# A 31-tap depthwise convolution in three blocks of a fused model: two of six channel chunks move to ScalarE and GpSimd

## The chip, the cores and the metric

The kernel runs on one core of one Trainium2 chip. The metric is the device time of one execution in microseconds. Before the change, three runs took 1864.44, 1865.39 and 1867.44 us, so the median is 1865.39 us. One further execution was taken with the hardware profiler; all rows below come from it.

## The reference, cut to what matters

The model is a chain of three blocks over a sequence of 256 tokens with 1024 channels, in float32. The change lies in the first half of the third block ("3a"), in its convolution mixer:

```
proj = h @ w_in
a    = proj[..., :768] + b_glu[:768]
gate = proj[..., 768:1536] + b_glu[768:]
q_mem = proj[..., 1536:]
u = a * sigmoid(gate)
c = depthwise_conv(pad_left(u, 30), dw_w) + dw_b     # 31 taps per channel, 768 channels
c = silu(layer_norm(c, ln_g, ln_b))
m = memory_attention(q_mem, memq_g, mem_k, mem_v)    # 4 heads of 64
x = x + concat(c, m) @ w_out
```

Each output channel of the convolution is the sum of 31 products, each of one channel of `u`, shifted by one to 31 tokens, with one weight of that channel. After it come a SwiGLU, then block 3b (sliding-window attention and a mixture of eight experts).

## The kernel before, in words

Activations lie with channels on the 128 partitions and tokens on the free axis; a tile is 128 x 2 x 256, two chunks of 128 channels. Weights stream from HBM into a ring of 1 MB buffers (`raw`, issued on SyncE's queue). For precise float32 products ScalarE (ACT) rounds a weight piece into `whi` (L305) and VectorE (DVE) subtracts it into `wlo` (L306); `mm3` (L325) makes three products of each pair. A piece has 1024 columns, and each of the two tags has four buffers.

The convolution's 768 channels are six chunks, (p, c) with p from 0 to 2 and c 0 or 1. `block3a` (L1122) runs over p: two linear layers make `a` and `gate` of the pair (L1153, L1155), ACT takes the sigmoid (L1163), DVE multiplies into `u` (tile `cu`, 32 columns of zeros ahead of 256). The 31 taps of a chunk are split:

- Taps 0 to 17 run on DVE in `taps` (L1140): the first is a `tensor_scalar` with the bias (L1148), each further one a `scalar_tensor_tensor` that reads the shifted `u` and the running sum `conv`, and writes the sum back (L1150). These are 18 dependent instructions per chunk, 108 in all.
- Taps 18 to 30 (`PE_TAPS = 13`) run on TensorE (PE): ACT scales the identity by the weight column into a 128 x 128 diagonal `dg` (L1181, six buffers, no dependence on the data), and PE multiplies `u` by it into the PSUM tile `cv` (L1182). These are 78 diagonals and 78 float32 products (two records each in the trace).
- DVE adds `cv` to `conv`, once for each p (L1186).

After that come the memory attention (L1187 and L1188), which needs nothing of the convolution, the mean over channels (`mu`, L1191), the subtraction (L1196), the variance, `rs` (L1203), the normalisation (L1208), SiLU (L1210), and the output projection (L1213), which begins with the memory attention's chunks.

The order of the instructions on each engine isn't written out. A list scheduler orders them at compile time: of the instructions that it holds to be ready, an engine takes the one that was written first in the program, by the scheduler's own estimate of durations. On the chip every engine then runs its list in that order, and an instruction that waits holds up all that are behind it. The tiles of `bpool_tile` (L591) come from a pool of four buffers, 128 x 2 x 288.

GpSimd (POOL) has 30 instructions in the whole kernel: fills of constants and zeros, and a few DMA issues.

Of the kernel before, what the change touches and what calls it, by code (L numbers as in the profile page):

```python
# [15 lines left out]
AF = mybir.ActivationFunctionType  # L16
OP = mybir.AluOpType
# [10 lines left out]
GROUPS = ((0,), (1,), (2, 3), (4, 5), (6, 7))  # L28
TAGS = ("u", "u", "x2", "u", "x2")
HEAD = 2  # L30
PE_TAPS = 13
EARLY = 7
PRE = 2
KEEP = (0, 72, 81)
# [174 lines left out]
class Build:  # L209
# [912 lines left out]
    def block3a(self):  # L1122
        nc, a = self.nc, self.a
        gg = self.small("gg", 8)
        nc.vector.tensor_tensor(gg, self.col("fin_g", 0, 8), self.col("cv_g", 0, 8), op=OP.mult)
        h = self.gained(self.x, lambda c: gg[:, c:c + 1])
        rs1 = self.rms_row(self.sum_sq(self.x), "rs1")
        acc = self.sum_sq(self.x, lambda c: self.col("fin_g", c))
        for i in range(2):
            nc.vector.tensor_tensor(acc, acc, rs1, op=OP.mult)  # L1130
        rs = self.rms_row(acc)
        for j in range(4):
            for c in range(2):
                nc.vector.scalar_tensor_tensor(self.x[j][:, c, :], self.x[j][:, c, :], self.col("fin_g", 2 * j + c),
                                               rs1, op0=OP.mult, op1=OP.mult)
        nc.vector.tensor_tensor(rs, rs, rs1, op=OP.mult)
        w = a["cv_w_in"]
        us, cs, todo = [], [], []

        def taps(n):  # L1140

            for _ in range(min(n, len(todo))):
                p, c, j = todo.pop(0)
                cc = 2 * p + c
                src, o = us[p][:, c, j + 2:j + 258], cs[p][:, c, :]
                wc = self.col("dw_w", cc * 31 + j)
                if j == 0:
                    nc.vector.tensor_scalar(o, src, wc, self.col("dw_b", cc), op0=OP.mult, op1=OP.add)  # L1148
                else:
                    nc.vector.scalar_tensor_tensor(o, src, wc, o, op0=OP.mult, op1=OP.add)  # L1150

        for p in range(3):
            pa_ = self.linear(w, 2 * p, h)  # L1153
            taps(EARLY)
            pg = self.linear(w, 2 * p + 1, h)  # L1155
            u = self.bpool_tile("cu")
            nc.gpsimd.memset(u[:, :, 0:32], 0.0)
            sg = self.stile("sg").rearrange("p (a b) -> p a b", a=2)
            self.scaled(sg, pg, rs)
            self.scaled(u[:, :, 32:288], pa_, rs)  # L1160
            for c in range(2):
                cc = 2 * p + c
                self.gate_act(sg[:, c, :], sg[:, c, :], AF.Sigmoid, bias=self.col("glu_b", 6 + cc))  # L1163
                nc.vector.scalar_tensor_tensor(u[:, c, 32:288], u[:, c, 32:288], self.col("glu_b", cc), sg[:, c, :],
                                               op0=OP.add, op1=OP.mult)
            us.append(u)
            cs.append(self.unit("conv"))
            todo += [(p, c, j) for c in range(2) for j in range(31 - PE_TAPS)]
            taps(EARLY)
        pq = self.linear(w, 6, h)  # L1170
        q = self.unit("mq")
        self.scaled(q, pq, rs)
        self.exp_set()
        for p in range(3):
            t = cs[p]
            pc = self.pb("cv")
            for c in range(2):
                cc = 2 * p + c
                for i, j in enumerate(range(31 - PE_TAPS, 31)):
                    dg = self.medium("dg")  # L1180
                    nc.scalar.activation(dg, self.con("ident"), AF.Copy, scale=self.col("dw_w", cc * 31 + j))  # L1181
                    nc.tensor.matmul(pc[:, c * 256:(c + 1) * 256], dg, us[p][:, c, j + 2:j + 258], start=i == 0,  # L1182
                                     stop=i == PE_TAPS - 1, skip_group_check=True)
                while todo and todo[0][:2] <= (p, c):
                    taps(1)
            nc.vector.tensor_tensor(t, t, pc.rearrange("p (a b) -> p a b", a=2), op=OP.add)  # L1186
        self.head_rms(q.rearrange("p a b -> p (a b)"), q, self.g8[:, 0:1])  # L1187
        om = self.mem_attention(q)  # L1188
        pm = self.pa("mu")
        for cc in range(6):  # L1190
            self.stats_mm(pm, cs[cc // 2][:, cc % 2, :], cc == 0, cc == 5)  # L1191
        mu = self.stile("mu", 256)
        nc.scalar.activation(mu, pm[:, :256], AF.Copy, scale=1.0 / 768)
        pv = self.pa("var")
        for p in range(3):
            nc.vector.tensor_tensor(cs[p], cs[p], mu.rearrange("p (a b) -> p a b", a=1).to_broadcast([128, 2, 256]),  # L1196
                                    op=OP.subtract)
            sq = self.stile("sq")
            nc.scalar.activation(sq, cs[p].rearrange("p a b -> p (a b)"), AF.Square)
            for c in range(2):  # L1200
                self.stats_mm(pv, sq[:, c * 256:(c + 1) * 256], p == 0 and c == 0, p == 2 and c == 1)
        rs = self.stile("rs", 256)
        self.rsqrt(rs, pv[:, :256], 1.0 / 768, "e5")  # L1203
        act = []
        for p in range(3):
            for c in range(2):
                cc = 2 * p + c
                nc.vector.scalar_tensor_tensor(cs[p][:, c, :], cs[p][:, c, :], self.col("ln_g", cc), rs,  # L1208
                                               op0=OP.mult, op1=OP.mult)
                self.gate_act(cs[p][:, c, :], cs[p][:, c, :], AF.Silu, bias=self.col("ln_b", cc))  # L1210
            act.append(self.split(cs[p], "cn"))
        self.exp_set()
        self.out_proj(a["cv_w_out"], self.chunks([om]), self.chunks(act), self.add_x)  # L1213
        self.dump("x2b", self.x)
        h = self.gained(self.x, lambda c: self.col("cvf_g", c))
        rs = self.rms_row(self.sum_sq(self.x))
        f = []
        for j in range(11):
            pg = self.linear(a["cv_w_gate"], j, h)
            pu = self.linear(a["cv_w_up"], j, h)  # L1220
            t, v = (self.stile(n).rearrange("p (a b) -> p a b", a=2) for n in ("sg", "su"))
            self.scaled(t, pg, rs)
            self.gate_act(t, t, AF.Silu)
            self.scaled(v, pu, rs)
            nc.vector.tensor_tensor(t, t, v, op=OP.mult)
            f.append(self.split(t, "f", "u2" if j < 4 else "u"))
        self.exp_set()
        for j in range(4):
            self.add_x(j, self.linear(a["cv_w_down"], j, self.chunks(f)))
# [466 lines left out]
```

## Time and profile before

| What | Value |
|---|---|
| median of three runs | 1865.39 us |
| profiled execution, own time | 1858.88 us |
| its span | 1857.0 us |
| busy: PE, DVE, ACT, POOL | 1817.5, 1207.7, 960.9, 10.8 us |
| granted clock of TensorE over the span | 0.995 |
| convolution stretch, first tap on DVE to the last sum | 605.1 to 663.9 us |

The span is the time from the first to the last instruction in the profile; the execution's own time is 1.9 us longer. Busy shares are means over stages of different character: from 1060 us on, among the experts, the DMA engines are busy for 0.99 of the time, and in the convolution for 0.37 and 0.11.

### The profile page before, as it was taken

To read this page: it belongs to the slowest core of one execution; us is meant where nothing else is said; L and a number is where in the kernel's file an instruction comes from. 1 tells how busy PE (TensorE), PEld (TensorE's weight loads), DVE (VectorE), ACT (ScalarE), POOL (GpSimd) and SP (SyncE) were. 2 spreads that over 40 slices of the span, in tenths; PEclk is the share of its full clock that TensorE was granted. 3 is DMA by queue.
4 is the path that set the end of the run, shared out by engine and by line. 5 is a ranking of instruction groups with operands and counts; after the bars stand their busy time and mean duration, and the time that the engine had idled before them with its cause. 6 is when DMAs were issued, how large, how long until landed. Compare 5 with 4: busy or idle time off the path is not lost. (4 is left out here: it accounts for less than half of the span.)

```text
span 1857.0 us, 30774 instructions
## 1 busy us (share of the span) xinstructions
PE 1817.5 (98%) x12304; PEld 1505.6 (81%) x12304; DVE 1207.7 (65%) x1814; ACT 960.9 (52%) x1429; POOL 10.8 (1%) x30
## 2 busy tenths in 40 slices
PE   7999999999999999999998999999999999999997
PEld 7989998989999979999877766766676666676674
DVE  7689787666467977665577654656555655565563
ACT  5545555555455675454565644545454444444451
POOL 0000000000000000000000000000000000000000
PEclk9999999999999999999999999999999999999999
DMA  9766467345554215555524899999999999999995
GB/s 307 256 251 227 183 227 286 129 144 204 182 182 169 108 56 194 200 181 208 204 94 159 367 412 420 420 416 419 420 421 417 421 419 420 420 415 420 421 420 223
DMA packets 77655, 531.29 MB, mean 286 GB/s; under 512 B 9283, under 2 KB 10051, under 8 KB 15425
## 3 DMA queue, kind: packets, MB, share of 16 engines
q1 hardware_dynamic: 75168, 524.66, 71.7%
q0 software_dynamic: 1328, 3.29, 0.9%
q8 instruction: 98, 1.61, 0.3%
q10 hardware_dynamic: 1008, 1.31, 0.2%
q14 instruction: 53, 0.43, 0.1%
HBM read 526.60 MB, written 2.62 MB: 285 GB/s over the span
## 5 line engine op out<-in xcount | busy, mean ns | idle before, releaser
L306 DVE TENSOR_TENSOR wlo<-raw,whi 128x1024 fp32r<-128x1024 f32 x618 | 726.8, 1204 | 327.7 <-ACT whi L305 325.1
L305 ACT ACTIVATE whi<-raw 128x1024 fp32r<-128x1024 f32 x618 | 625.8, 1042 | 362.6 <-PE lin L325 243.6
L325 PE MATMUL lin<-hh,whi 128*128 128x256 f32 x1248 | 355.5, 285 | 10.0 <-ACT whi L305 7.8
L325 PE MATMUL lin<-hh,wlo 128*128 128x256 f32 x1248 | 351.7, 282 | 1.8 <-DVE wlo L306 1.8
L325 PE MATMUL lin<-hl,whi 128*128 128x256 f32 x1248 | 352.7, 283 | 0.3
L325 PEld LDWEIGHTS lin<-hh,whi 128*128 128x128 f32 x1248 | 237.6, 190 | 14.9 <-ACT whi L305 8.8
L325 PEld LDWEIGHTS lin<-hh,wlo 128*128 128x128 f32 x1248 | 237.4, 190 | 4.0 <-DVE wlo L306 2.5
L325 PEld LDWEIGHTS lin<-hl,whi 128*128 128x128 f32 x1248 | 237.5, 190 | 2.7 <-issue 1.5
L1546 PE MATMUL g<-whi,xe 128*128 128x512 f32 x448 | 141.3, 396 | 0.0
L1546 PE MATMUL up<-whi,xe 128*128 128x512 f32 x448 | 139.3, 392 | 0.0
L1648 ACT ACTIVATE ah<-aT 128x512 fp32r<-128x512 f32 x28 | 16.7, 596 | 168.2 <-PE aT L1642 168.2
L1538 PE MATMUL up<-raw,xn 128*64 128x256 f32 x896 | 103.0, 380 | 0.0
L1538 PE MATMUL g<-raw,xn 128*64 128x256 f32 x896 | 102.9, 382 | 0.0
L1557 PE MATMUL y<-raw,an 128*64 128x512 f32 x448 | 102.3, 599 | 0.5 <-ACT an L1645 0.5
L1546 PEld LDWEIGHTS up<-whi,xe 128*128 128x128 f32 x448 | 84.2, 188 | 18.0
L1546 PEld LDWEIGHTS g<-whi,xe 128*128 128x128 f32 x448 | 82.1, 188 | 16.2
L1538 PEld LDWEIGHTS up<-raw,xn 128*64 128x64 f32 x896 | 63.6, 137 | 33.2 <-issue 1.4
L1569 PE MATMUL y<-whi,ah 128*128 128x512 f32 x224 | 90.3, 403 | 0.0
L289 ACT ACTIVATE act<-g,gs 128x512 f32<-128x512 f32 (+1 forms) x56 | 32.5, 581 | 111.5 <-PE g L1538 81.6
L1546 PE MATMUL g<-wlo,xe 128*128 128x512 f32 x224 | 89.2, 398 | 0.0
L1546 PE MATMUL up<-wlo,xe 128*128 128x512 f32 x224 | 89.2, 398 | 0.0
L1538 PEld LDWEIGHTS g<-raw,xn 128*64 128x64 f32 x896 | 61.8, 137 | 33.0 <-issue 3.8
(467 smaller groups left out, 3147.0 us busy)
## 6 DMA issues: line engine op xcount, KB each, us to landing
raw<-we_gate SPq DMA_DIRECT2D x112, 1024.0 KB, 11.0
raw<-we_up SPq DMA_DIRECT2D x112, 1024.0 KB, 11.5
raw<-we_down SPq DMA_DIRECT2D x112, 1024.0 KB, 11.8
raw<-w_in SPq DMA_DIRECT2D x35, 1024.0 KB, 6.1
raw<-w_ff SPq DMA_DIRECT2D x32, 1024.0 KB, 4.8
raw<-ada_w SPq DMA_DIRECT2D x24, 1024.0 KB, 4.9
raw<-cv_w_gate SPq DMA_DIRECT2D x11, 1024.0 KB, 4.8
raw<-cv_w_up SPq DMA_DIRECT2D x11, 1024.0 KB, 4.8
```

What stands on the lines that cost most here:

```text
L289: self.last_gate = self.nc.scalar.activation(*args, **kw)
L305: self.splits_done.append(nc.scalar.activation(hi[:, :w], raw[:, o:o + w], AF.Copy))
L306: self.low_done = nc.vector.tensor_tensor(lo[:, :w], raw[:, o:o + w], hi[:, :w].bitcast(F32), op=OP.subtract)
L325: nc.tensor.matmul(o, s, m, start=start and n == 0, stop=stop and n == 2, skip_group_check=True)
L1538: nc.tensor.matmul(ps[64 * h:64 * h + 64, 0:256], xe["N"][:, kk, :], raw[:, k * 512 + h * 256:k * 512 + (h + 1) * 256], start=kk == 0, sto ...
L1546: nc.tensor.matmul(ps, s, m, start=n == 0, stop=n == 23)
L1557: self.downs = nc.tensor.matmul(yp[0][64 * n:64 * n + 64, :], st, raw[:, k * 1024 + n * 512:k * 1024 + (n + 1) * 512], start=b == 0 and pa ...
L1569: self.downs = nc.tensor.matmul(yp[n], s, m, start=b == 0 and kk == 0 and q == 0, stop=b == 6 and kk == 3 and q == 2)
L1648: nc.scalar.activation(ah, pt, AF.Copy)
```

## The change

Chunks (0, 0) and (1, 0) leave both DVE and PE. For each of their 31 taps ACT makes the product of the shifted `u` and the weight column; the first goes with the bias straight into `conv`, the other 30 into one of two halves of a new tile `tap` (a fourth tile of the pool of four), and a GpSimd `tensor_tensor` adds that half to `conv`. The 31 pairs are written into the program right after the pair's `u` is made, ahead of the next linear layers. The other four chunks keep the old scheme with 10 taps on PE and 21 on DVE. The last sum (L1186) covers one chunk of two where p is 0 or 1.

```diff
-PE_TAPS = 13
+PE_TAPS = 10
+POOLED = ((0, 0), (1, 0))
...
+        def tap(p, c, j):
+            cc = 2 * p + c
+            return us[p][:, c, j + 2:j + 258], cs[p][:, c, :], self.col("dw_w", cc * 31 + j), self.col("dw_b", cc)
+
+        spare = self.bpool_tile("tap")
+
+        def sums(p, c, j):
+
+            src, o, wc, bc = tap(p, c, j)
+            if j == 0:
+                nc.scalar.activation(o, src, AF.Identity, scale=wc, bias=bc)
+                return
+            t = spare[:, j % 2, 0:256]
+            nc.scalar.activation(t, src, AF.Copy, scale=wc)
+            nc.gpsimd.tensor_tensor(o, o, t, op=OP.add)
...
-            todo += [(p, c, j) for c in range(2) for j in range(31 - PE_TAPS)]
+            for c in range(2):
+                if (p, c) in POOLED:
+                    for j in range(31):
+                        sums(p, c, j)
+                else:
+                    todo += [(p, c, j) for j in range(31 - PE_TAPS)]
...
-            for c in range(2):
+            mine = [c for c in range(2) if (p, c) not in POOLED]
+            for c in mine:
...
-            nc.vector.tensor_tensor(t, t, pc.rearrange("p (a b) -> p a b", a=2), op=OP.add)
+            nc.vector.tensor_tensor(t[:, mine[0]:, :], t[:, mine[0]:, :],
+                                    pc.rearrange("p (a b) -> p a b", a=2)[:, mine[0]:, :], op=OP.add)
```

## Rows read from the trace of the kernel before

**Rows 1.** Busy time of each engine in stretches of block 3a (from and to in us from the span's start, the length, then the busy us of each engine with its instructions, the granted clock of TensorE, the DMA engines' share and GB/s).

```profile
core 0: us, PE busy (x) PEld busy (x) DVE busy (x) ACT busy (x) POOL busy (x), PEclk, DMA share, GB/s
605.00:632.10 27.10, 27.10 (x220) 26.54 (x219) 26.99 (x54) 13.48 (x21) 0.00 (x0) 1.00 0.37 134
632.10:663.90 31.80, 31.80 (x150) 27.85 (x149) 31.80 (x78) 26.85 (x68) 0.00 (x0) 1.00 0.11 45
663.90:681.00 17.10, 15.09 (x73) 9.41 (x71) 8.44 (x26) 10.56 (x29) 0.00 (x0) 1.00 0.18 62
```

**Rows 2.** DVE's instructions in order of time (start, length of the run, line, operation, count).

```profile
594.05 1.22 DVE L306 TENSOR_TENSOR wlo<-raw,whi 128x1024 fp32r<-128x1024 f32 x1
...
595.18 0.42 DVE L399 TENSOR_TENSOR acc<-acc 128x256 f32<-128x256 f32 x1
595.52 0.48 DVE L1134 SCALAR_TENSOR_TENSOR x<-x,cols,rs 128x256 f32<-128x256 f32 x1
...
605.09 0.73 DVE L1148 TENSOR_SCALAR conv<-cu,cols 128x256 f32<-128x256 f32 x2
...
652.62 0.67 DVE L1186 TENSOR_TENSOR conv<-conv,cv 128x512 f32<-128x512 f32 x1
653.22 9.57 DVE L1150 SCALAR_TENSOR_TENSOR conv<-cu,cols,conv 128x256 f32<-128x256 f32 x24
...
663.32 0.67 DVE L1186 TENSOR_TENSOR conv<-conv,cv 128x512 f32<-128x512 f32 x1
```

**Rows 3.** Groups of instructions from 605 to 664 us by line and engine (busy us and mean ns, then idle time before them).

```profile
L1150 DVE SCALAR_TENSOR_TENSOR conv<-cu,cols,conv 128x256 f32<-128x256 f32 x102 | 42.0, 472 | 0.1
L1182 PE MATMUL cv<-cu,dg 128*128 128x256 f32 x156 | 34.0, 378 | 0.0
...
L1148 DVE TENSOR_SCALAR conv<-cu,cols 128x256 f32<-128x256 f32 x6 | 2.2, 403 | 0.0
```

**Rows 4.** PE's instructions of the convolution and the first ones after it, in order of time.

```profile
618.15 3.18 PE L1182 MATMUL cv<-cu,dg 128*128 128x256 f32 x14
...
632.11 30.83 PE L1182 MATMUL cv<-cu,dg 128*128 128x256 f32 x142
662.77 1.03 PE L1067 MATMUL st<-sq,consts 128*128 128x256 f32 x4
663.63 2.32 PE L367 MATMUL mu<-conv,consts 128*128 128x256 f32 x10
...
667.10 0.70 PE L367 MATMUL mu<-conv,consts 128*128 128x256 f32 x2
```

**Rows 5.** ACT in order of time: two products with a weight column (the operation nearest to the new ones), six diagonals that wait for nothing, and the diagonals of the convolution.

```profile
12.11 0.89 ACT L429 ACTIVATE hh<-x,cols 128x256 fp32r<-128x256 f32 x2
12.91 1.84 ACT L1181 ACTIVATE dg<-consts,cols 128x128 f32<-128x128 f32 x6
...
618.78 2.99 ACT L1181 ACTIVATE dg<-consts,cols 128x128 f32<-128x128 f32 x7
...
632.74 0.83 ACT L1181 ACTIVATE dg<-consts,cols 128x128 f32<-128x128 f32 x2
...
634.00 26.78 ACT L1181 ACTIVATE dg<-consts,cols 128x128 f32<-128x128 f32 x63
```

**Rows 6.** All fills of GpSimd by shape (busy us and mean ns of one).

```profile
L1516 POOL MEMSET selT<- 128x512 f32 x4 | 2.1, 526 | 868.5 <-PE ht L1436 397.9 <-PE cmb L1664 240.3 <-PE up L1538 230.2
...
L1157 POOL MEMSET cu<- 128x64 f32 x3 | 0.5, 174 | 66.7 <-DVE p L748 66.7
L802 POOL MEMSET va<- 128x2 f32 x4 | 0.3, 102 | 38.7 <-issue 37.2 <-PE bdp L783 1.6
```

**Rows 7.** One of these fills and what DVE ran at that moment; the last line is a run of DVE with no GpSimd instruction beside it.

```profile
1228.10 0.53 POOL L1516 MEMSET selT<- 128x512 f32 x1 [178.79 <-PE up L1538]
...
1226.07 4.63 DVE L306 TENSOR_TENSOR wlo<-raw,whi 128x1024 fp32r<-128x1024 f32 x4 [3.75 <-ACT whi L305]
...
691.28 2.35 DVE L306 TENSOR_TENSOR wlo<-raw,whi 128x1024 fp32r<-128x1024 f32 x2
```

**Rows 8.** Waits from 605 to 632 us, longest first (us in total, times, longest).

```profile
ACT whi L305 <- PE lin L325: 11.1, 6, 2.2
```

**Rows 9.** The way from the convolution to the output projection, on DVE and ACT in order of time.

```profile
669.79 0.39 ACT L1193 ACTIVATE mu<-mu 128x256 f32<-128x256 f32 x1
...
671.41 0.68 DVE L1196 TENSOR_TENSOR conv<-conv,mu 128x512 f32<-128x512 f32 x1
...
673.87 0.68 DVE L1196 TENSOR_TENSOR conv<-conv,mu 128x512 f32<-128x512 f32 x1
...
676.47 0.62 ACT L1199 ACTIVATE sq<-conv 128x512 f32<-128x512 f32 x1
...
680.25 0.60 ACT L268 ACTIVATE omh<-po 128x512 fp32r<-128x512 f32 x1 [0.53 <-PE po L1118]
...
681.49 2.46 DVE L1208 SCALAR_TENSOR_TENSOR conv<-conv,cols,rs 128x256 f32<-128x256 f32 x6
```

**Rows 10.** The stages behind: two stretches of the experts by engine (columns as in rows 1), and what SyncE's queue waited for from 600 to 1000 us (us in total, times, longest).

```profile
1000.00:1020.00 20.00, 16.72 (x87) 13.81 (x85) 17.37 (x48) 13.18 (x18) 0.00 (x0) 0.95 0.43 158
...
1060.00:1857.00 797.00, 782.08 (x4414) 538.66 (x4412) 440.77 (x480) 368.95 (x457) 1.05 (x2) 1.00 0.99 407
...
SPq L281 <- DVE wlo L306: 367.8, 58, 34.1
```

More of the change, by code (lines that the diff above doesn't have):

```diff
@@ L1143, in taps @@
                 p, c, j = todo.pop(0)
-                cc = 2 * p + c
-                src, o = us[p][:, c, j + 2:j + 258], cs[p][:, c, :]
-                wc = self.col("dw_w", cc * 31 + j)
+                src, o, wc, bc = tap(p, c, j)
                 if j == 0:
-                    nc.vector.tensor_scalar(o, src, wc, self.col("dw_b", cc), op0=OP.mult, op1=OP.add)
+                    nc.vector.tensor_scalar(o, src, wc, bc, op0=OP.mult, op1=OP.add)
                 else:
```

## The prediction

> **What bounds the kernel now.** I read the busy times by stretch first. From 605 to 663.9 us, from the first tap on VectorE (DVE) to the last sum, DVE is busy for 58.8 of 58.9 us [rows 1]: it is the clock of this stretch. TensorE (PE) is full as well: up to 632.1 us with the linear layers, then with the convolution's products, which end at 662.9 us [rows 1, 4]. ScalarE (ACT) is busy for 13.5 of 27.1 us and then 26.9 of 31.8 us; GpSimd (POOL) does nothing. Next come the groups: 102 + 6 of DVE's instructions are taps (44 us busy), and they have no idle time before them [rows 3]. Then the time order: DVE's taps run back to back to 662.8 us and the last sum ends at 664.0 us [rows 2]. Behind it a chain of short steps on all engines (memory attention, mean, variance) leads to the output projection at about 681 us, with DVE busy for 8.4 of 17.1 us [rows 1, 9]. So whatever moves DVE's end in this stretch moves all that follows. Later stages pass a shift on: SyncE's queue waits for `wlo` (368 us from 600 to 1000 us), so loads start when earlier work frees their buffers, and they shift along with it, also into the part where the DMA engines are busy for 0.99 of the time [rows 10].
>
> **The change part by part.**
>
> *DVE, removed.* Taps go from 6 x 18 to 4 x 21, that is 22 `scalar_tensor_tensor` and 2 `tensor_scalar` fewer. 24 of the first kind take 9.57 us; with 0.47 us for the last one the step is (9.57 - 0.47) / 23 = 0.396 us, and 22 are 8.7 us. The second kind steps at 0.73 - 0.40 = 0.33 us, two are 0.65 us. Two of the three sums shrink to half: a whole one steps at 653.22 - 652.62 = 0.60 us, a 128x256 `tensor_tensor` at 595.52 - 595.18 = 0.34 us, so 0.5 us goes [rows 2, 3]. Together **9.9 us** off a full engine.
>
> *PE, removed.* 38 taps of two records each; 142 records take 30.83 us, 0.217 us each, so 76 are 16.5 us [rows 4]. PE would be done at about 646 us, before DVE (653 to 654 us at best), so this brings nothing beyond DVE's 9.9 us; what is late next is DVE's own list.
>
> *ACT, changed.* Two products of 128x256 with a weight column take 12.11 to 12.91 us, 0.40 us each; 62 are 24.8 us. Diagonals that wait for nothing take 1.84 / 6 = 0.31 us; 63 of them took 26.78 us because they wait for PE [rows 5]. Of ACT's 40.3 busy us from 605 to 663.9 us the diagonals are 2.99 + 0.83 + 26.78 = 30.6, the rest 9.7 us [rows 1, 5]. After it: 9.7 + 34 x 0.31 + 24.8 = 45 us, in the 49 us that would be left at best. It fits with little room. ACT's idle time up to 632 us is a wait for a free `whi` buffer (11.1 us in six waits) [rows 8], and the weight pieces run ahead of PE, so a product between two pieces costs nothing as long as it isn't itself held up.
>
> *POOL, added.* 60 adds in one dependent chain, which can begin after 605.8 us. No row shows a GpSimd instruction that reads a tensor. The nearest are fills: 0.102 us for 2 elements, 0.526 us for 512, so 0.10 us to start and 0.83 ns per element of one stream, 0.21 us for 256 [rows 6]. An add has two streams in and one out: 0.31 us if they run beside each other, 0.10 + 3 x 0.21 = 0.74 us if one after the other. 60 x 0.74 = 44 us, so the chain alone would end at about 650 us and be hidden under DVE's taps.
>
> *What an add costs DVE.* This decides the case. DVE's taps and `wlo` read two tensors from SBUF, as the add does, and run without a gap, so anything that an add takes from DVE shows in full. The bounds are 0 and the whole add, 0.74 us; below nothing is left out, since an add can't shorten a tap. The only row with both engines is a fill: while it wrote for 0.53 us, four `wlo` took 4.63 us; a single one lasts 1.22 us, so they stepped at (4.63 - 1.22) / 3 = 1.14 us, against 595.18 - 594.05 = 1.13 us and 2.35 - 1.22 = 1.13 us with GpSimd idle [rows 2, 7]. Writing costs DVE nothing, then. I therefore leave out the write and charge the rest, the start and the two reads: 0.10 + 2 x 0.21 = **0.53 us** per add, 31.8 us for 60. The change breaks even at 9.9 / 60 = 0.165 us per add; of the span from 0 to 0.74, 78% lies above it.
>
> The Trainium skill ("SBUF — State Buffer", section "Who interferes with whom") says that a DVE instruction with two SBUF inputs contends with a GpSimd instruction that reads SBUF but not with one that only writes, and that the loser is blocked for the whole instruction. The trace agrees with the half on writes (1.14 against 1.13 us) and shows nothing of the half on reads. By that rule an add costs DVE its whole length. The Trainium skill ("GPSIMD Engine Reference", section "Performance versus the Vector engine") gives 4497 ns for a float32 add of 2048 elements; as an estimate from that page 256 would take 562 ns, and the sum would be 60 x 0.56 - 9.9 = +24 us.
>
> *The sum.* 31.8 - 9.9 = +21.9 us on DVE, whose last sum moves from 664 to 686 us. Each add would also wait for the DVE instruction that is running, 0.40 us or more, a pace of 0.74 + 0.40 = 1.14 us, and the 60 adds would end at 605.8 + 68 = 674 us, while DVE is still full, so all of them count. ACT is held in order: a product waits until the add two before it has freed its half of `tap`, and behind it wait weight pieces and diagonals. PE then idles some time in a stretch that had none; that is inside the DVE sum. The fourth tile of the pool of four costs nothing: its slots' earlier users lie in the first two blocks (the fills of `cu` waited for L748, and the fourth is the tile of block 2's rotary table) [rows 6]. The profiled execution took 1858.9 us (span 1857.0 and 1.9 around it), so 1880.8 us; the median of the runs shown lies 6.5 us higher, so **1887 us**.
>
> **The rivals.**
>
> *The adds cost DVE nothing.* Then the change does what it says: DVE ends 9.9 us earlier, PE and POOL are done before it, ACT just fits: 1865.4 - 9.9 = 1855.5 us (1853 to 1859, as ACT's order fits worse or better). For it: the fill beside `wlo` [rows 7]. Against it: the fill reads nothing. It decides below 0.165 us per add. Chance 0.25.
>
> *GpSimd's own pace becomes the bound.* DVE isn't slowed, but an add and its hand-over with ACT take more than about 0.95 us, so that 605.8 + 60 x 0.95 = 663 us is where DVE ended before. At 1.14 us (0.74, and 0.40 us for a product that couldn't start ahead) the chain ends at 674 us. The mean then takes 2.3 + 0.7 us on PE, and from it to the normalisation there are at least 0.39 + 3 x 0.60 + 0.62 and the variance with its `rs`, 5 us in all, and at most the 13.7 us of today (667.8 to 681.5 us, where the memory attention is woven in) [rows 4, 9]: 682 to 691 us against 681.5 us, so 0 to +9 us, 1865 to 1874 us, middle 1869 us. For it: the two halves of `tap` let ACT run at most two products ahead, and ACT has 45 us of other work in between. Against it: the fills put an add at 0.74 us at most. Chance 0.12.
>
> *GpSimd is the one that is blocked.* DVE keeps its step and ends at 654 us, but the adds pass only in DVE's gaps; ACT's products, and behind them the weight pieces that DVE needs, wait for them, so that DVE gets its gaps by force. The sum of both engines' work is the same. This is inside the forecast, at its lower end.
>
> **How the numbers follow.** A measurement of this kernel can tell about 0.2%, 3.7 us, from no change. The forecast (sharing decides) has a chance of 0.60. Its own range goes from 0.30 us per add (+8 us, 1873 us) to the whole 0.74 us (+34.5 us, 1900 us); it counts as slower but for 0.02. The first rival is faster but for 0.01, the second is even at 0.06, slower at 0.05 and faster at 0.01. What is left, 0.03, is a new order of instructions in the stages around, mostly slower, at 1870 us. That makes 0.26 faster, 0.10 same, 0.64 slower. The range of 8 in 10 holds both signs: 1854 to 1897 us. Below it lies a small part of the first rival, above it the adds that cost their full length or more.
>
> **What would show it.** Right: taps on DVE that last well over 0.47 us, or gaps between them, while adds run; the last sum near 686 us; adds longer than 0.74 us in places; products on ACT waiting for GpSimd. Wrong: taps that still step at 0.396 us with adds beside them, which means the first rival if the last sum comes at 654 us, the second if `mu` waits for an add. A step that grows by less than 0.165 us per add would prove the mechanism and still turn the sign. A granted clock of TensorE below 1.00 in the stretch would add a cost that I haven't priced.

## The result, and the profile after

The changed kernel takes 1879.3 us (median of 4 runs, 1875.58 to 1881.6); the kernel before, in 4 runs beside it, 1864.91 us. The medians are 14.4 us apart. The ratio of the two is put at 1.0069 (12.9 us), with a 95% interval from 1.0053 to 1.0085: the kernel became slower. 1887.0 us were predicted, with a range from 1854 to 1897 us. The profiled execution took 1875.58 us (span 1873.8), which is 16.7 us more than the one before. That is 2.3 us more than between the medians, because the profiled execution of before lay 6.0 us under its median and this one 3.7 us.

Busy time by stretch in the changed kernel (columns as in rows 1):

```profile
604.50:632.00 27.50, 21.72 (x171) 20.89 (x170) 27.40 (x37) 18.25 (x34) 17.87 (x21) 0.97 0.20 68
632.00:664.00 32.00, 20.35 (x78) 13.53 (x76) 31.89 (x39) 22.41 (x49) 27.60 (x34) 0.71 0.27 99
664.00:681.30 17.30, 13.89 (x48) 10.29 (x48) 17.19 (x33) 12.42 (x31) 6.25 (x9) 0.79 0.07 12
```

DVE is full to 681.3 us, as it was to 663.9 us before [rows 1], although it has 24 taps less. PE, full before, is idle for 11.6 of 32 us. It has nothing to run from 625.6 to 631.3 us, and within that time its granted clock falls from 1.00 (2.4 GHz) to 0.50 (1.2 GHz); the 0.71 and 0.79 above are means of these two levels.

The same stretch by groups (busy us and mean ns of one, then idle time before them):

```profile
L1165 DVE SCALAR_TENSOR_TENSOR conv<-cu,cols,conv 128x256 f32<-128x256 f32 x80 | 55.6, 746 | 0.3
L1155 POOL TENSOR_TENSOR conv<-conv,tap 128x256 f32<-128x256 f32 x60 | 50.7, 845 | 247.8 <-ACT tap L1154 243.5
L1154 ACT ACTIVATE tap<-cu,cols 128x256 f32<-128x256 f32 x60 | 29.9, 506 | 13.2 <-POOL conv L1155 12.3
L1203 PE MATMUL cv<-cu,dg 128*128 128x256 f32 x80 | 27.6, 487 | 12.5 <-ACT dg L1202 12.5
```

A tap takes 746 ns in the mean, against 472 [rows 3]: 80 taps are busy for longer than 102 were. Idle time stands before the products (12.3 us, they wait for adds) and before PE's taps (12.5 us, they wait for diagonals), none before DVE's.

DVE and POOL in order of time (start, length of the run, count):

```profile
604.53 0.42 DVE L1163 TENSOR_SCALAR conv<-cu,cols 128x256 f32<-128x256 f32 x1
...
605.38 1.76 DVE L307 TENSOR_TENSOR wlo<-raw,whi 128x1024 fp32r<-128x1024 f32 x1
...
618.85 11.02 DVE L1165 SCALAR_TENSOR_TENSOR conv<-cu,cols,conv 128x256 f32<-128x256 f32 x13
...
655.21 0.81 DVE L1163 TENSOR_SCALAR conv<-cu,cols 128x256 f32<-128x256 f32 x1
655.95 15.59 DVE L1165 SCALAR_TENSOR_TENSOR conv<-cu,cols,conv 128x256 f32<-128x256 f32 x20
...
671.79 7.18 DVE L1165 SCALAR_TENSOR_TENSOR conv<-cu,cols,conv 128x256 f32<-128x256 f32 x17
...
680.62 0.68 DVE L1207 TENSOR_TENSOR conv<-conv,cv 128x512 f32<-128x512 f32 x1
...
636.01 33.66 POOL L1155 TENSOR_TENSOR conv<-conv,tap 128x256 f32<-128x256 f32 x37 [1.97 <-ACT tap L1154]
```

The adds end at 636.01 + 33.66 = 669.7 us. Up to there the taps are long: 20 of them take 15.59 us. Behind it 17 take 7.18 us, which is 7.18 - 0.47 over 16, a step of 0.42 us, near the 0.396 us of before [rows 2].

One add and one tap by themselves show what happens:

```profile
657.62 0.79 POOL L1155 TENSOR_TENSOR conv<-conv,tap 128x256 f32<-128x256 f32 x1
657.75 0.95 DVE L1165 SCALAR_TENSOR_TENSOR conv<-cu,cols,conv 128x256 f32<-128x256 f32 x1
```

The add ends at 658.41 us and the tap at 658.70 us. Instruction by instruction the trace has 45 taps that began while an add ran and lasted over 0.55 us; every one of them ended 0.28 us after that add. An add takes 0.79 us and the next one starts 0.08 us later, so one tap passes per add: a step of 0.87 us in place of 0.396 us, 0.47 us for each tap that is held.

From the first tap to the last sum there are 681.30 - 604.53 = 76.8 us, against 58.9 us. The output projection then begins at 698.7 us against 680.9 us before, so the shift passes on whole: the way from the last sum to it takes 17.4 us, and took 17.0 us.

### The profile page after: what moved, and what is told of

The parts are those of the page before. It is cut to its first block, busy times and chain, and to the rows that moved or that the text cites. A ratio compares the mean times of both kernels' runs of the same rounds, so it can differ in the third digit from the quotient of the medians.

```text
span 1873.8 us, 30741 instructions
## 1 busy us (share of the span) xinstructions
PE 1813.5 (97%) x12228; PEld 1494.7 (80%) x12228; DVE 1225.2 (65%) x1790; ACT 973.7 (52%) x1453; POOL 61.5 (3%) x90
## 5 line engine op out<-in xcount | busy, mean ns | idle before, releaser
L1670 ACT ACTIVATE ah<-aT 128x512 fp32r<-128x512 f32 x28 | 16.7, 596 | 168.2 <-PE aT L1664 168.2
```

What stands on the lines that cost most here:

```text
L1670: nc.scalar.activation(ah, pt, AF.Copy)
```

## The experiments

The kernel before had a median of 1865.4 us beside the first four experiments, 1868.8 us beside the next four, and 1866.8 us beside the last three. Each ratio compares an experiment with the kernel before beside it.

**Fills in place of adds.** The changed kernel, with each add replaced by two fills of the half of `tap`; the sums of two chunks keep their first tap only.

```diff
-            nc.gpsimd.tensor_tensor(o, o, t, op=OP.add)
+            for _ in range(2):
+                nc.gpsimd.memset(t, 0.0)
```

> The changed kernel, but each of the 60 adds is replaced by two fills of the same half of `tap` (zeros, 128x256 each), so GpSimd writes and reads nothing, while ACT still waits for it; the two chunks keep only their first tap. Sharing theory (an add that reads SBUF holds up DVE's instructions with two SBUF inputs, 0.45 us each): DVE's taps step at 0.40 us again beside a busy GpSimd, the last sum comes 8 to 10 us earlier than in the kernel before, and the time is 7 to 10 us below the kernel before (about 0.995). Queue theory (ACT's products wait for GpSimd in order, and weight pieces and diagonals wait behind them): the waits stay, GpSimd's two fills last about 0.62 us, and the time stays 8 to 15 us above the kernel before.

Measured: 1856.88 us, ratio 0.9947 [0.9924, 0.997] (it moves as many bytes as the kernel before, 531.3 MB in all, so the time can be compared). DVE and POOL in order of time:

```profile
618.94 5.22 DVE L1166 SCALAR_TENSOR_TENSOR conv<-cu,cols,conv 128x256 f32<-128x256 f32 x13
...
643.13 13.00 DVE L1166 SCALAR_TENSOR_TENSOR conv<-cu,cols,conv 128x256 f32<-128x256 f32 x32
656.24 0.69 DVE L1208 TENSOR_TENSOR conv<-conv,cv 128x512 f32<-128x512 f32 x1
656.84 1.82 DVE L307 TENSOR_TENSOR wlo<-raw,whi 128x1024 fp32r<-128x1024 f32 x2
...
615.86 4.76 POOL L1156 MEMSET tap<- 128x256 f32 x14 [0.88 <-ACT tap L1154]
```

Thirteen taps that took 11.02 us beside adds take 5.22 us beside fills, (5.22 - 0.47) / 12 = 0.396 us each. The stretch lasts 656.93 - 607.45 = 49.5 us; the prediction's sum without a price for the adds is 58.9 - 9.9 = 49.0 us. The adds therefore cost 76.8 - 49.5 = 27.3 us, **0.455 us each**. The two stretches don't hold quite the same: here 1.7 us of `wlo` come behind the last sum, and DVE waits 1.1 us for ACT and PE. That is 0.7 us between them, 0.01 us per add.

**Idle adds, and idle fills.** The kernel before, with 60 adds on GpSimd that nothing uses, no products on ACT, and the taps of PE and DVE as they were; and the same with 118 fills and two one-input products.

```diff
+            if p < 2:
+                for j in range(1, 31):
+                    s = spare[:, 0, 0:256]
+                    nc.gpsimd.tensor_tensor(s, s, u[:, 0, j + 2:j + 258], op=OP.add)
```

> The kernel before with its whole convolution, and 60 adds on GpSimd beside it (30 after u of p = 0, 30 after u of p = 1) that read `u` and a scratch tile and whose sum nobody uses. ACT, PE and DVE have the same instructions in the same order as before. Sharing theory: each add costs DVE about 0.45 us, DVE's last sum comes 60 x 0.45 = 27 us later, and the time rises by 22 to 28 us (1.012 to 1.015). Queue theory: nobody waits for these adds, so the time stays (1.000 within 0.002).

> The same as the run before, with 120 fills of 128x256 on GpSimd in the place of the 60 adds (the first of each of the two groups is a product with zero, so that it starts after u). Sharing theory with the page's distinction between reading and writing: fills cost DVE nothing, the taps step at 0.40 us, and the time stays (1.000 within 0.002). If any busy GpSimd holds DVE up, the time rises by 20 us or more, as with the adds. Queue theory: 1.000.

Measured: 1892.39 us, ratio 1.0143 [1.0111, 1.0174] with adds, and 1868.13 us, 1.0008 [0.9993, 1.0022] with fills. With adds:

```profile
606.30 56.18 POOL L1173 TENSOR_TENSOR tap<-tap,cu 128x256 f32<-128x256 f32 x60 [234.60 <-DVE cu L1166]
...
613.10 1.76 DVE L306 TENSOR_TENSOR wlo<-raw,whi 128x1024 fp32r<-128x1024 f32 x1
...
624.87 9.23 DVE L1152 SCALAR_TENSOR_TENSOR conv<-cu,cols,conv 128x256 f32<-128x256 f32 x11
...
667.24 6.41 DVE L1152 SCALAR_TENSOR_TENSOR conv<-cu,cols,conv 128x256 f32<-128x256 f32 x16
```

With fills:

```profile
608.46 21.75 POOL L1173 MEMSET tap<- 128x256 f32 x59
...
618.63 4.44 DVE L1151 SCALAR_TENSOR_TENSOR conv<-cu,cols,conv 128x256 f32<-128x256 f32 x11
```

Eleven taps take 9.23 us beside adds, 4.44 us beside fills; once the adds have ended at 662.5 us, 16 take 6.41 us, a step of 0.396 us. A queue on ACT can't be the cause, since ACT has nothing of it here. The stretch is 83.1 us long (606.47 to 689.56 us), 24.2 us more than before, 0.40 us per add. The tap's step beside adds is the same as in the changed kernel, (9.23 - 0.47) / 10 = 0.88 us.

**The running sums in PSUM.** The changed kernel, with DVE's running sums in PSUM up to each chunk's last tap, so that a tap has one tensor operand in SBUF.

```diff
-                    nc.vector.scalar_tensor_tensor(o, src, wc, o, op0=OP.mult, op1=OP.add)
+                    nc.vector.scalar_tensor_tensor(o if j == 30 - PE_TAPS else s, src, wc, s, op0=OP.mult, op1=OP.add)
```

> The changed kernel, but DVE's running sums lie in two PSUM banks that the memory attention uses later; only the last tap of a chunk writes to SBUF. A tap on DVE then reads one tensor from SBUF and one from PSUM. Sharing theory: taps are no longer held up (0.40 us beside the adds, only `wlo` and the first taps still are), the last sum comes 6 to 10 us earlier than in the kernel before, and the time is 3 to 9 us below it (0.995 to 0.998). Queue theory: it stays near the changed kernel's 1.007, since ACT's order and the number of adds are as there.

Measured: 1883.65 us, ratio 1.0096 [1.0069, 1.0122], a miss. DVE, POOL, and PE's longest wait (us in total, times, longest):

```profile
647.67 0.42 DVE L1214 TENSOR_TENSOR conv<-conv,cv 128x256 f32<-128x256 f32 x1 [3.74 <-PE cv L1210]
648.01 8.71 DVE L1172 SCALAR_TENSOR_TENSOR acc<-cu,cols,acc 128x256 f32<-128x256 f32 x22
...
663.81 0.42 DVE L1214 TENSOR_TENSOR conv<-conv,cv 128x256 f32<-128x256 f32 x1 [6.31 <-PE cv L1210]
...
640.98 27.17 POOL L1161 TENSOR_TENSOR conv<-conv,tap 128x256 f32<-128x256 f32 x33 [0.21 <-ACT tap L1160]
...
PE cv L1210 <- ACT dg L1209: 14.4, 15, 7.4
```

The sharing is gone: 22 taps beside adds take 8.71 us, 0.39 us each. But DVE now waits for PE's products, 3.74 and 6.31 us, and PE waits 14.4 us for diagonals, which stand on ACT behind products that wait for adds. At 27.17 / 33 = 0.82 us a piece the adds still end at 668.2 us. So the adds' own pace, which the prediction's second rival named, comes next behind the first cause; but it acts through ACT's list, and not at `mu`, where PE waits for an add for 0.5 us only.

**One chunk instead of two.** PE keeps 13 taps of five chunks; the sums once in PSUM (first) and once in SBUF.

```diff
-PE_TAPS = 10
-POOLED = ((0, 0), (1, 0))
+PE_TAPS = 13
+POOLED = ((0, 0),)
```

> One chunk of six, (0, 0), goes to ACT and GpSimd (30 adds), PE keeps 13 taps of the other five, and DVE's running sums lie in PSUM. Theory now (an add holds a DVE instruction with SBUF operands alone for 0.45 us, and ACT's and GpSimd's chain is the next bound behind it): DVE has 18 taps less, 18 x 0.396 = 7.1 us; 30 adds at the 0.8 us seen with sums in PSUM take 24 us and end by about 632 us, far ahead of the last sum; they hold only the weight remainders wlo and the like, 2 to 4 us. So DVE's last sum at 659 to 661 us in place of 664.0 and a ratio to the kernel before of 0.997 to 0.999. If the chain of products and adds is the bound even with half the adds: the last sum where it was or later, ratio 1.000 to 1.005. If sums in PSUM cost something by themselves (the running sum no longer than in SBUF so far, but with a longer wait): DVE's taps over 0.40 us per step.

> The same with one chunk of six on ACT and GpSimd, and DVE's running sums in SBUF as in the changed kernel. Sharing at 0.45 us per add: 30 x 0.45 - 7.1 = +6 us, ratio 1.002 to 1.005, taps that step near 0.87 us until the adds end and at 0.396 us after. If what costs in the changed kernel is ACT's and GpSimd's chain (60 links that end too late), 30 links end by 640 us and cost nothing: ratio 0.996 to 0.998. Beside the run with sums in PSUM the difference is the price of sharing alone.

Measured: 1867.9 us, ratio 1.0 [0.9984, 1.0016] with PSUM; 1870.66 us, 1.002 [1.0004, 1.0037] with SBUF. DVE with PSUM:

```profile
615.67 5.57 DVE L1171 SCALAR_TENSOR_TENSOR acc<-cu,cols,acc 128x256 f32<-128x256 f32 x14
...
630.74 0.91 DVE L1185 SCALAR_TENSOR_TENSOR cu<-cu,cols,sg 128x256 f32<-128x256 f32 x1 [6.74 <-ACT sg L290]
```

And with SBUF:

```profile
620.50 11.86 DVE L1165 SCALAR_TENSOR_TENSOR conv<-cu,cols,conv 128x256 f32<-128x256 f32 x14
```

Fourteen taps take 5.57 or 11.86 us, for the same adds beside them. With SBUF the expectation held. With PSUM the taps were free as expected, but DVE idled for 6.74 us waiting for a sigmoid. ACT's list has up to five products between two weight pieces, and each waits about 0.3 us for an add. The sigmoid stands behind them, and so does a diagonal for which PE waits 4.7 of its 6.8 idle us from 605 to 632 us. That is about as much as the 7.1 us gained.

**What a read costs.** The kernel before with 60 idle products that read one tensor.

```diff
+                    nc.gpsimd.tensor_scalar(spare[:, 0, 0:256], u[:, 0, j + 2:j + 258], 0.5, None, op0=OP.mult)
```

> The kernel before, and 60 idle GpSimd products with a constant that read one SBUF tensor of 128x256 and write one (nothing uses them). If GpSimd holds DVE for a fixed part of each instruction that reads, whatever it reads: 0.4 to 0.5 us each, +24 to +28 us, ratio about 1.014 as with the idle adds. If the price goes by the streams that it reads, half of the add's: +10 to +15 us, ratio 1.006 to 1.008. If only instructions with two tensor inputs count: taps at their 0.396 us step, ratio 1.000.

Measured: 1876.26 us, ratio 1.0038 [1.0023, 1.0053]. The groups from 604 to 673 us on DVE, and the one on POOL:

```profile
L1151 DVE SCALAR_TENSOR_TENSOR conv<-cu,cols,conv 128x256 f32<-128x256 f32 x102 | 48.3, 535 | 0.1
...
L1171 POOL TENSOR_SCALAR tap<-cu 128x256 f32<-128x256 f32 x60 | 57.2, 953 | 421.2 <-DVE cu L1165 416.4
```

All three numbers expected missed. 0.0038 x 1869 us = 7.1 us are 0.12 us per instruction; the stretch (605.03 to 672.02 us) says 0.13 us. It isn't the length that counts, since these products last 953 ns in the mean, longer than an add, nor half a price for half the reads. One product and one tap:

```profile
640.65 0.85 POOL L1171 TENSOR_SCALAR tap<-cu 128x256 f32<-128x256 f32 x1
640.71 0.61 DVE L1151 SCALAR_TENSOR_TENSOR conv<-cu,cols,conv 128x256 f32<-128x256 f32 x1
```

The tap ends at 641.32 us, before the product does at 641.50 us. So it is for all 45 taps that are held here, by 0.17 to 0.18 us, where a tap beside an add ended 0.28 us after it.

**Idle adds beside sums in PSUM.** The 60 idle adds again, with the sums in PSUM.

> The kernel before with the same 60 idle adds on GpSimd as in the earlier run (1.0143 there) and DVE's running sums in PSUM. Sharing between SBUF operands alone: DVE's taps keep their step of 0.396 us, the adds hold only wlo, the gate's products and the tensor_scalar instructions, 5 to 8 us in all, ratio 1.002 to 1.005. If DVE's taps are held because they read u in SBUF at all, or because the adds read the same tile u: still +20 us or more, ratio over 1.010.

Measured: 1877.44 us, ratio 1.0042 [1.0027, 1.0057], as expected and 0.0101 below the same adds beside sums in SBUF.

```profile
643.34 11.05 DVE L1157 SCALAR_TENSOR_TENSOR acc<-cu,cols,acc 128x256 f32<-128x256 f32 x28
...
606.40 53.90 POOL L1179 TENSOR_TENSOR tap<-tap,cu 128x256 f32<-128x256 f32 x60 [234.17 <-DVE cu L1171]
```

28 taps take 11.05 us with adds beside them that read the same `u`: a shared tile isn't what holds a tap, its second operand in SBUF is.

**Without ACT's products.** The changed kernel and the one with sums in PSUM, with adds that read `u` itself; the weights of two chunks are left out. That changes the router's choices, more expert weights are read (885 MB in place of 531 MB), and the execution takes some 860 us more. The ratios of 1.4619 and 1.4599 say nothing, then, and only the stretch is read.

```diff
-            t = spare[:, j % 2, 0:256]
-            nc.scalar.activation(t, src, AF.Copy, scale=wc)
-            nc.gpsimd.tensor_tensor(o, o, t, op=OP.add)
+            nc.gpsimd.tensor_tensor(o, o, src, op=OP.add)
```

> The changed kernel without ACT's products: the 60 adds read the shifted u itself (the weights of two chunks are left out), so no add waits for ACT and ACT is 24.8 us lighter. If an add holds DVE for 0.40 to 0.45 us whoever feeds it: 58.9 - 9.9 + 60 x 0.40 to 0.45 = 73 to 76 us from DVE's first tap to its last sum, ratio to the kernel before of 1.004 to 1.008, hardly better than the changed kernel (1.0069). If ACT's queue is what makes the changed kernel slow: the stretch at 50 to 60 us and a ratio of 0.995 to 0.999.

> The same without ACT's products, and DVE's running sums in PSUM, as in the earlier run that came out at 1.0096. There I read the loss as ACT's products holding up weight pieces and diagonals. If so, this one has neither sharing nor the queue: taps at 0.396 us, adds at 0.73 to 0.80 us that end near 655 us, no wait of DVE for cv above 1 us, the normalisation (the six instructions with rs) starting at 672 to 680 us in place of 681.5, ratio 0.995 to 0.999. If the sums in PSUM, or the new order of instructions that they bring, cost time by themselves: ratio 1.003 or more although no engine waits for ACT's products.

The first, sums in SBUF:

```profile
605.64 56.40 POOL L1152 TENSOR_TENSOR conv<-conv,cu 128x256 f32<-128x256 f32 x60 [402.07 <-ACT conv L1150]
...
623.29 10.87 DVE L1162 SCALAR_TENSOR_TENSOR conv<-cu,cols,conv 128x256 f32<-128x256 f32 x13
...
662.45 12.74 DVE L1162 SCALAR_TENSOR_TENSOR conv<-cu,cols,conv 128x256 f32<-128x256 f32 x32
...
679.81 0.68 DVE L1204 TENSOR_TENSOR conv<-conv,cv 128x512 f32<-128x512 f32 x1
```

The stretch lasts 680.49 - 605.30 = 75.2 us, inside the 73 to 76 us expected of sharing and 1.6 us below the changed kernel's. But it holds 2.4 us that come behind the last sum in the changed kernel: 1.7 us of the memory attention's instructions and 0.8 us of waiting for it. Without them it is 72.8 us, and (72.8 - 49.0) / 60 = 0.40 us per add, as for the idle adds. ACT's products are thus worth 1.6 to 4 us of the 27.3 us. In the changed kernel DVE waits for them nowhere; what differs is how many taps the adds meet: 47 last over 0.55 us in the changed kernel, 38 here and 38 beside idle adds.

The second, sums in PSUM (the last line is PE's):

```profile
607.07 53.99 POOL L1158 TENSOR_TENSOR conv<-conv,cu 128x256 f32<-128x256 f32 x60 [403.35 <-ACT conv L1156]
...
635.59 10.27 DVE L1169 SCALAR_TENSOR_TENSOR acc<-cu,cols,acc 128x256 f32<-128x256 f32 x26
...
665.23 0.42 DVE L486 TENSOR_REDUCE st<-sc 128x1 f32<-128x256 f32 x1 [12.12 <-PE sc L1103]
...
661.12 2.08 PE L368 MATMUL mu<-conv,consts 128*128 128x256 f32 x4 [11.51 <-POOL conv L1158]
```

Neither sharing on the taps nor the queue is left, no wait of DVE for `cv` either, and yet the normalisation begins at 692.6 us, not at the 672 to 680 us expected: a miss. PE stands at `mu` for 11.5 us because the last add ends at 661.06 us; memory attention is behind it in PE's list, and DVE waits 12.1 us for that, with 17 of its taps behind in its own list. The chain of adds, at 0.90 us each, ends 2.9 us before the kernel before had its last sum (663.99 us), so the chain alone isn't the bound: the orders of PE's and DVE's lists make it one.

**One chunk, written later.** The run with one chunk and PSUM, its products and adds moved in the program behind the linear layers.

> One chunk on ACT and GpSimd with DVE's sums in PSUM, as in the run that came out at 1.000, and the 31 products and adds written into the program behind the linear layers in place of ahead of them, so that of what is ready ACT prefers weight pieces and sigmoids. In the run at 1.000 PE was idle for 7 of 27 us and DVE for 6.7 us because weight pieces and sigmoids stood behind products that waited for adds. If that ate the 7 us: DVE's wait gone or below 3 us, last sum at 659 to 664 us, ratio 0.996 to 0.998. If the order on ACT stays much the same (there are still four to six products between two weight pieces): ratio 0.999 to 1.001.

Measured: 1881.1 us, ratio 1.0072 [1.0056, 1.0089]: a miss, and worse than where they stood.

```profile
635.52 1.02 DVE L1185 SCALAR_TENSOR_TENSOR cu<-cu,cols,sg 128x256 f32<-128x256 f32 x2 [5.40 <-ACT sg L290]
...
646.69 0.69 DVE L439 SCALAR_TENSOR_TENSOR mq<-lin,rsr 128x512 f32<-128x512 f32 x1 [3.31 <-PE lin L326]
```

The waits of DVE for ACT and PE stayed. The same instructions in another order are 13 us apart, so what one chunk is worth is decided by the order of the engines' lists. ACT's has a part in it; no run separates it from the others. No version that computes the whole convolution beats the kernel before.

## Why the prediction was right, and where its sizes were off

**The mechanism held.** An add takes time from DVE's taps, DVE is full, and the loss shows whole. Fills in the adds' place bring the step of 0.396 us back, idle adds take it away again, and a tap without a second SBUF operand isn't held. The first rival (adds are free) falls with the first of these. The second (GpSimd's pace is the bound) falls with the changed kernel's own trace: the adds end 11.6 us before the last sum, and DVE waits for nothing. ACT's products are worth 1.6 to 4 us of the 27.3 us, from the run without them. That GpSimd is the one blocked is not so either: an add grows from 0.727 us beside sums in PSUM to 0.790 us in the median, a tap from 0.47 to 0.95 us.

**The mis-sized term is the price of an add: "the start and the two reads: 0.10 + 2 x 0.21 = 0.53 us per add".** It measured 0.455 us in place (0.40 us for idle adds, 0.40 to 0.43 us without products). 60 x (0.53 - 0.455) = 4.5 us: nearly the 5.2 us by which the profiled execution stayed under the sum, 1875.58 against 1880.8 us. The rest of the 7.7 us to the median is that this profile lay 3.7 us under its median, where the 6.5 us of before were added. The working behind the term is refuted though the size is near, so the nearness is luck: it prices a read at 0.21 us and the start at 0.10, so a one-input instruction would cost 0.31 us, and it costs 0.12 to 0.13 us. What the trace shows in its place is a tap held to the add's end, one per add, for the adds' pace less the tap's own step: 0.87 - 0.396 = 0.47 us.

**Which instructions are held.** The Trainium skill ("SBUF — State Buffer", section "Who interferes with whom") names the instructions that were held beside adds: those with two SBUF inputs, as taps and `wlo` (1.76 against 1.22 us), and, as one that can be, `tensor_scalar` (0.81 against 0.42 us). The runs agree, and also in what it excepts: two-input instructions beside fills, and taps with an operand in PSUM. The Trainium skill ("SBUF — State Buffer", section "Summary: rules for kernel authors") says that the second of the two to issue is fully blocked until the first finishes. For adds the trace agrees: the held taps end 0.28 us after the add. The prediction took from this that an add costs DVE its whole length; that doesn't follow, since the next add has begun before the held tap ends. For products with one tensor the trace doesn't agree: the held taps end 0.17 us before the product does.

**The other steps.** The 9.9 us taken off DVE: near (49.5 us measured for 49.0; 8.8 us off when the `wlo` behind the last sum is counted in and the waits are left out). An add of 0.31 to 0.74 us: at the upper end, 0.727 us for the shortest. Their pace of 1.14 us: too slow, (669.7 - 605.3) / 60 = 1.07 us over all, but 33.66 / 37 = 0.91 us in the steady part, since a tap lengthens an add by 0.06 us in the median and not by 0.40 us. Their end at 674 us came at 669.7 us, the last sum at 681.3 us and not 686 us. "PE then idles some time ... inside the DVE sum" held in the changed kernel, where DVE has no wait; with the sums in PSUM the same waits set the time. "ACT just fits", said for the first rival, held beside fills, where DVE waits 1.1 us in the stretch. Beside adds ACT has the time (45.4 busy us from 604.5 to 669.7 us) but not the order, as the waits with sums in PSUM show. TensorE's clock, unpriced, fell to 0.71; PE was idle beside it, and DVE waited for PE nowhere in the stretch. What the clock cost behind it isn't separated; the way to the output projection grew by 0.4 us in all.

## What to carry to other kernels

An elementwise add on GpSimd isn't free beside a VectorE that reads two SBUF tensors: compare its price on VectorE (here 0.455 us) with what it relieves VectorE of before anything else. Here that was 9.9 us in 60 adds, 0.165 us each, since 62 more taps on ScalarE are, on balance, 24 fewer on VectorE and 38 fewer on TensorE; even a tap of 0.396 us off VectorE for each add wouldn't have paid. An operand in PSUM takes VectorE out of the conflict, but then the next bound counts: the chain of dependent adds at 0.8 to 0.9 us each, through the in-order lists of the engines that feed it and wait for it. An idle copy of the suspected instruction, added to the old kernel, prices such sharing in one run.

## What was unexpected

A GpSimd instruction with one tensor input cost VectorE 0.12 us although it lasted 0.953 us; an add of 0.73 to 0.79 us, with two inputs, cost 0.40 to 0.455 us. The traces show where the difference lies: a tap beside an add is held until the add has ended, a tap beside a product is let go before the product ends. No run here shows why.
